# Scaling the inputs of two output projections by their RMS-norm factor ahead of the matmul, and adding the products to x from PSUM

## The chip, the cores and the metric

The kernel runs on one core of one Trainium2 chip. The metric is the device time of one execution in microseconds (us). The engines are PE (TensorE, matmul), DVE (VectorE), ACT (ScalarE), POOL (GpSimd) and SP (SyncE, which issues most DMAs).

## What is computed

The reference is one inference step of a decoder trunk with two layers, for a prompt of 512 tokens and 8 samples of 4 tokens (544 columns in all), with a model width of 1024. What matters here is the mixing part of a layer:

```python
a = window_attention(q, k_ext, v_ext, sinks, pos0)          # 512 wide
c = causal_depthwise(u_ext, w_dw, b_dw)                     # 512 wide
c = jax.nn.silu(layernorm(c, ln_g, ln_b)) @ w_pw2
mix = jnp.concatenate([rmsnorm(a, g_attn_out), rmsnorm(c, g_conv_out)], axis=-1) @ w_o
x = x + mix
x = x + jnp.square(jax.nn.relu(rmsnorm(x, g_ffn) @ w_up)) @ w_down
x = x + (p @ w_ple) * jax.nn.sigmoid(rmsnorm(x, g_ple) @ w_ple_gate)
```

An RMS norm multiplies every token by one factor, the reciprocal root of its mean square, and every feature by a gain. The factor of a token can be applied ahead of the matmul that follows or behind it, since the matmul sums over features only.

## The kernel before

Everything is held with features on the 128 partitions and the 544 tokens along the free dimension: x is eight tiles of 128x544, the attention output `aT` and the output `cn` of the pointwise product are four tiles each. The matmuls work in fp32r, and to keep fp32 accuracy each operand is split in a high and a low part; `split` (L584) makes a tile `pr` of both: ACT writes the high part (scaled by the gain, when one is given), DVE writes the rest. `group` (L567) multiplies one block of 128 output features by all input tiles: for each input tile three matmuls (high x high, high x low, low x high) for each of two halves of 288 and 256 columns, which accumulate in two PSUM banks. With four input tiles that is 24 matmuls. Weights are loaded 512 KB at a time by SP; ACT makes their high part and the negative of it, and a DMA issued by POOL adds the raw weights, or DVE subtracts (L493).

`rstd` (L613) makes the norm factor: the squares (ACT) are summed over tiles by DVE or POOL (`sqsum`, L594), PE sums over partitions with a matmul against ones, DVE scales (TENSOR_SCALAR t<-bank), POOL takes the power -0.5 (t<-t,mhalf), PE broadcasts the result over partitions (bank<-ident,t), and ACT copies it to a tile of 128x544 in two pieces (448 and 96 columns).

The stages of a layer that the change touches are, in the code: `an` (L954: splits of the four attention tiles with the gain, and the factor Ra), `oa` (L957: the projection of the attention half, eight groups), `ln` and `pw` (L966, L983: layer norm, SiLU, pointwise product, whose four groups give `cn`), `cn` (L991: splits of `cn` and the factor Rc), `oc` (L994: the projection of the convolution half, eight groups), and then `ffn` (L1003). In `oa` and `oc` each group's two banks are multiplied by the factor into a half tile (`mulR`, L683), and a further DVE addition of 128x544 adds the half tile to x. `addx` (L695) adds two banks to x directly; in this kernel nothing calls it yet.

The order of the instructions on each engine isn't the order of the code. `Program` (L155) records operations with their dependences and a duration, and `schedule` (L207) is a list planner: at each point in its own time it starts on every free engine the ready operation with the smallest key, if its buffers are free. The key is the place of the operation's section in `ORDERS` (L36, one list for each layer) and then the order of recording; evacuations of PSUM recorded while `first` is set go ahead of all others. An operation counts as ready 0.13 us after the last one that it depends on (L358). The chip then takes the planned order of each engine as it is. In layer 0 the list has pw and cn ahead of an, ln, ple and oa, with oc and ffn behind; in layer 1 it has ln and pw ahead of an, then cn, ple, oa, oc, ffn. Section ple is a product of a small embedding input with its own weights, independent of the rest of the layer.

Since every instruction is issued by one helper, all rows carry the line L1143, and groups are told apart by tile names: `pr` split inputs, `hfs` half tiles, `bank` PSUM, `raw`, `wh`, `wl` weights, `par` the gains, `fa`, `fb`, `fc`, `C`, `tq` and `hg` the forms of ffn, `t` small tiles.

Of the kernel before, what the change touches and what calls it, by code (L numbers as in the profile page):

```python
# [12 lines left out]
ALU = mybir.AluOpType  # L13
# [42 lines left out]
SQ = {"hr": "dd", "sp": [2, 4], "an": "pd", "ln": "dp", "cn": "pp"}  # L56
BC = {"hr": [0, 0], "an": [0, 0], "cn": [0, 0], "ffn": [0, 0], "gate": [0, 0]}
W0B = 1
ENG = {"d": "dve", "p": "pool", "m": "dma"}
KINDS = set(SLOTS) | {"hf"}  # L60

# [93 lines left out]
class Program:  # L155
# [51 lines left out]
    def schedule(self):  # L207
# [84 lines left out]
        t = 0.0  # L292
        left_ops = len(self.ops)
        while left_ops:
            while events and events[0][0] <= t:
                _, _, o = heapq.heappop(events)
# [5 lines left out]
            for e in engs:  # L302
                w, h = wait[e], heap[e]
                while w and w[0][0] <= t:
                    _, p, i, o = heapq.heappop(w)
# [15 lines left out]
                o = pick  # L321
# [33 lines left out]
                heapq.heappush(events, (o.end, id(o), o))  # L355
                for s in o.succ:
                    s.n -= 1
                    s.ready = max(s.ready, o.end + (0.0 if s.eng == e == "pe" else 0.13))  # L358
                    if s.n == 0:
                        heapq.heappush(wait[s.eng], (s.ready, s.key, id(s), s))  # L360
                progress = True
# [13 lines left out]
            t = min(nxt)  # L375
# [4 lines left out]
class Kernel:  # L380
# [131 lines left out]
    def quad(self, l, idx, F, how, taps):  # L512
# [10 lines left out]
        whole = slice(0, 1024)  # L523
        conv(p, whole, {4: a, 1: b}, ENG[how[0]])
        self.tt(p[:, a], p[:, a], q[:, a], ALU.add)
        self.tt(q[:, a], q[:, a], p[:, b], ALU.add)
        self.tt(p[:, b], p[:, b], p[:, a], ALU.add)
        conv(p, whole, {5: a, 6: b}, ENG[how[1]])
        conv(q, b, {2: b}, ENG[how[2]])
        self.tt(q[:, b], q[:, b], p[:, b], ALU.add)  # L530
        conv(q, whole, {7: a, 3: b}, ENG[how[3]])
        bank = {}
# [61 lines left out]
    def sqsum(self, tiles, cols=slice(0, T), parts=1, eng="d", split=0):  # L594
        def chain(ts, e):
            s = None
            for a in ts:
# [4 lines left out]
                else:  # L602
                    self.tt(s[:, cols], s[:, cols], q[:, cols], ALU.add, ENG[e])
            return s
# [75 lines left out]
    def record(self):  # L680
        i, o, pg = self.i, self.o, self.pg

        def mulR(out, pv, r):  # L683
            pg.first = EVAC
            for h in range(2):
                self.tt(out[:, HS[h]], pv[h], r[:, HS[h]], ALU.mult)
            pg.first = False
# [7 lines left out]
        def addx(xm, pv):  # L695
            pg.first = EVAC
            for h in range(2):
                self.tt(xm[:, HS[h]], pv[h], xm[:, HS[h]], ALU.add)
            pg.first = False

        def const(name, shape):
            t = self.fixed(shape, name)
            self.dma(t, i[name])
            return t
# [9 lines left out]
        x = [self.fixed([128, T], "x") for _ in range(KD)]  # L714
        self.dma(par[0][:, 0:8], i["par"][0][:, 0:8])
        first = [self.sb("raw", [128, 1024], F32, "raw") for _ in range(2)]
        after = {0: (0, 0), W0B: (0, 1), KD - 1: (1, 0)}
        for k in range(KD):
            self.dma(x[k], i["xT"][:, k, :])
            if k in after:  # L720
                n, c = after[k]
# [11 lines left out]
        for l in range(L):  # L733
            t = self.fixed([128, NH], "sinkp")
# [4 lines left out]
            t = self.fixed([128, 2], "sinks")  # L739
# [8 lines left out]
        for l in range(L):  # L748
            def sec(name):
                pg.sec(name, l)  # L750
# [3 lines left out]
            g_a, g_c, b_dw, ln_g, ln_b = (P[:, 24 + 4 * n:28 + 4 * n] for n in range(5))  # L754
# [19 lines left out]
            for c in range(4):  # L774
# [8 lines left out]
                t = self.hf()  # L783
# [68 lines left out]
            aT = []  # L852
            for t in range(4):
                sec(f"q{t}")
                q32 = rope(10 + t, 0.125)
                for g in range(2):
                    r = slice(64 * g, 64 * g + 64)
# [9 lines left out]
                for n in range(4):  # L867
# [4 lines left out]
                    for g in range(2):  # L872
                        if n % 2 == 0:
                            S[g] = self.ps1()
                        r = slice(64 * g, 64 * g + 64)
# [5 lines left out]
                for g in range(2):  # L881
# [3 lines left out]
                    for bp in range(2):  # L885
# [3 lines left out]
                        for d in range(nn):  # L889
                            blk, n = bp * 2 + d // 2, bp * 2 + d // 2 + d % 2  # L890
                            src = 0 if n == 0 else 2 * n - 1 + (blk - n + 1)
# [41 lines left out]
            for g in range(2):  # L933
                r = slice(64 * g, 64 * g + 64)
# [10 lines left out]
            for q in range(2):  # L945
                for w in self.weights(l, LD_PLE + q, 4, 2):
                    pv = self.group(w, pa)
                    t = self.hf()
# [3 lines left out]
                    pp.append(d)  # L952

            sec("an")  # L954
            aa = [self.split(aT[t], g_a[:, t:t + 1]) for t in range(4)]
            Ra = self.rstd(self.sqsum(aT, eng=SQ["an"][l]), 512, dma=BC["an"][l])
            sec("oa")  # L957
            for q in range(4):
                for m, w in enumerate(self.weights(l, LD_OA + q, 2, 4)):
                    pv = self.group(w, aa)  # L960
                    t = self.hf()
                    mulR(t, pv, Ra)
                    xm = x[2 * q + m]
                    self.tt(xm, t, xm, ALU.add)

            sec("ln")  # L966
            mu = self.ps2()
# [7 lines left out]
            for c in range(4):  # L975
                t = self.hf()
# [7 lines left out]
            cn = []  # L984
            for q in range(2):
                for w in self.weights(l, LD_PW + q, 2, 4):
                    pv = self.group(w, sa)
                    t = self.hf()
                    copy(t, pv)
                    cn.append(t)  # L990
            sec("cn")  # L991
            ca = [self.split(cn[c], g_c[:, c:c + 1]) for c in range(4)]
            Rc = self.rstd(self.sqsum(cn, eng=SQ["cn"][l]), DC, dma=BC["cn"][l])
            sec("oc")  # L994
            for q in range(4):
                for m, w in enumerate(self.weights(l, LD_OC + q, 2, 4)):
                    pv = self.group(w, ca)
                    t = self.hf()
                    mulR(t, pv, Rc)
                    xm = x[2 * q + m]  # L1000
                    self.tt(xm, t, xm, ALU.add)

            sec("ffn")  # L1003
            F, odd = {}, [None]
# [6 lines left out]
            for c in range(CHUNKS):  # L1011
                G = {}
                for k in range(4):
                    s, C = (self.sb("pair", [128, 4, TH], F32, n) for n in ("s", "C"))
# [52 lines left out]
            for hs in ((0,), (1,)) if last else ((0, 1),):  # L1067
                for m in range(8):
                    pv = self.group(ws[m] if last else self.weights(l, LD_GATE + m, 1, KD)[0], h, hs)
                    t = self.hf()  # L1070
# [205 lines left out]
```

## Time and profile before

| | us |
|---|---|
| median of 3 runs | 1254.72 |
| lowest and highest | 1251.88, 1254.75 |
| the profiled execution | 1254.24 |
| its span | 1252.5 |
| PE busy | 1205.1 |
| DVE busy | 1057.9 |
| ACT busy | 884.3 |
| POOL busy | 286.9 |

The mean granted clock of the profiled execution is 0.987. The span runs from the first to the last instruction; times in all rows below count from its start. A row of the groups gives engine, operation, output<-inputs, shapes and count, then busy time and the mean duration of one in ns, then the idle time of the engine ahead of it and what ended that. A row of the windows gives a stretch and its length, then busy time (and number of instructions) of PE, PEld, DVE, ACT and POOL (an engine without any is left out when the view is restricted to one tile), the granted clock, the share of the DMA engines and GB/s. A row of the time line gives start, duration, instruction and, in brackets, the idle time just before it and what ended it. Matmuls overlap in the pipeline: their mean duration is about 290 ns, but in a full stretch about 200 of them start in 25 us.

### The profile page before, as it was taken

The page shows a single profiled execution, that of the slowest core. Times are in us where ns is not written, and L with a number is a line of the kernel's source. Part 1 is how long each engine was busy: PE and PEld are TensorE (multiplying, and loading weights), DVE is VectorE, ACT ScalarE, POOL GpSimd, SP SyncE. Part 2 cuts the span into 40 slices and gives each one's busy share as a digit, 9 for nine tenths or more (in the row PEclk, how much of TensorE's full clock was granted, in tenths as well). Part 3 has the DMA queues.
Part 4 walks back from the last instruction along what each step waited for, and adds up shares of the span by engine and source line. Part 5 has one row for each costly group of instructions (what it writes and reads, how often), then busy time and mean ns, then how long its engine had stood idle before and what let it go on. Part 6 is the DMA issues. An engine that isn't in the chain of part 4 may idle for free.

```text
span 1252.5 us, 24414 instructions
## 1 busy us (share of the span) xinstructions
PE 1205.1 (96%) x9424; PEld 1177.4 (94%) x9424; DVE 1057.9 (84%) x2024; ACT 884.3 (71%) x1464; POOL 286.9 (23%) x296
## 2 busy tenths in 40 slices
PE   6998999999999999999999999999999999999997
PEld 6997899999999999999999979999999999999996
DVE  4999976999798897986559997798979979979855
ACT  7777886785775865857757688787758568577752
POOL 1747233110101101102147802201111011010111
PEclk8999999999999999999999999998999999999998
DMA  9895456285866858869979825535687587697862
GB/s 279 209 266 137 113 122 142 49 203 142 208 156 159 212 137 195 185 214 248 231 200 205 190 75 142 123 85 120 162 200 176 143 201 172 153 205 192 201 153 72
DMA packets 69701, 212.23 MB, mean 169 GB/s; under 512 B 11736, under 2 KB 16088, under 8 KB 69584
## 3 DMA queue, kind: packets, MB, share of 16 engines
q0 software_dynamic: 23328, 84.95, 36.6%
q1 hardware_dynamic: 46256, 125.72, 31.3%
q8 instruction: 74, 1.21, 0.4%
q14 instruction: 43, 0.35, 0.1%
HBM read 115.42 MB, written 10.28 MB: 100 GB/s over the span
## 4 chain that ended last, share of the span: by engine, by line
PE 48%; DVE 28%; issue 8%; DMA 8%; ACT 6%; POOL 1%; SPq 0%; DVEq 0%; POOLq 0%; ACTq 0%
PE bank L1143 48%; DVE bank L1143 6%; DMA wl<-raw 5%; DVE hfs L1143 5%; DMA raw<-wall 3%; DVE fb L1143 3%; DVE C L1143 3%; DVE raw L1143 2%; DVE tq L1143 2%; DVE wl L1143 2%; ACT wh L1143 2%; DVE x L1143 1%; ACT wl L1143 1%; DVE P L1143 1%; ACT hfs L1143 1%
## 5 line engine op out<-in xcount | busy, mean ns | idle before, releaser
L1143 PE MATMUL bank<-fb,wh 128*128 128x272 f32 x3072 | 585.6, 289 | 2.8 <-DVE fb L1143 1.7
L1143 PEld LDWEIGHTS bank<-fb,wh 128*128 128x128 f32 x3072 | 482.9, 189 | 5.8 <-DVE fb L1143 2.8
L1143 PE MATMUL bank<-fb,wl 128*128 128x272 f32 x1536 | 443.4, 289 | 8.4 <-DMA wl<-raw 5.7
L1143 ACT ACTIVATE wh<-raw 128x1024 fp32r<-128x1024 f32 (+1 forms) x326 | 312.7, 966 | 174.8 <-PE bank L1143 98.6
L1143 PE MATMUL bank<-pr,wh 128*128 128x256 f32 (+1 forms) x2176 | 425.1, 294 | 6.4 <-ACT wh L1143 6.0
L1143 PEld LDWEIGHTS bank<-pr,wh 128*128 128x128 f32 x2176 | 346.2, 191 | 11.7 <-ACT wh L1143 6.0
L1143 POOL DMA_DIRECT2D wl<-raw x162 | 141.1, 873 | 826.9 <-ACT wl L1143 610.4
L1143 PE MATMUL bank<-pr,wl 128*128 128x288 f32 (+1 forms) x1088 | 315.0, 290 | 1.3 <-DMA wl<-raw 1.3
L1143 PEld LDWEIGHTS bank<-fb,wl 128*128 128x128 f32 x1536 | 290.1, 189 | 10.1 <-DMA wl<-raw 6.8
L1143 PEld LDWEIGHTS bank<-pr,wl 128*128 128x128 f32 x1088 | 206.9, 190 | 1.9 <-DMA wl<-raw 1.7
L1143 DVE TENSOR_TENSOR wl<-raw,wh 128x1024 fp32r<-128x1024 f32 (+1 forms) x164 | 163.4, 998 | 23.5 <-PE bank L1143 15.0
L1143 ACT ACTIVATE wl<-raw 128x1024 fp32r<-128x1024 f32 x162 | 170.0, 1049 | 4.1 <-DVE raw L1143 4.0
L1143 DVE TENSOR_TENSOR raw<-raw,raw 128x512 f32<-128x512 f32 x192 | 130.8, 683 | 1.1
L1143 DVE SCALAR_TENSOR_TENSOR bank<-U,par,bank 128x512 f32<-128x512 f32 x176 | 126.9, 746 | 2.1 <-ACT bank L1143 0.8
L1143 DVE TENSOR_TENSOR x<-x,bank 128x272 f32<-128x272 f32 (+1 forms) x224 | 102.7, 470 | 29.5 <-PE bank L1143 29.0
L1143 POOL TENSOR_TENSOR hfs<-hfs,hfs 128x512 f32<-128x512 f32 (+3 forms) x74 | 101.0, 1367 | 48.7 <-ACT hfs L1143 23.0
L1143 PE MATMUL bank<-fa,wh 128*128 128x272 f32 x512 | 102.6, 292 | 1.7 <-DVE fa L1143 1.7
L1143 DVE TENSOR_TENSOR hfs<-bank,hfs 128x256 f32<-128x256 f32 (+2 forms) x160 | 65.9, 445 | 41.4 <-PE bank L1143 23.5
L1143 PEld LDWEIGHTS bank<-fa,wh 128*128 128x128 f32 x512 | 81.7, 190 | 3.3 <-DVE fa L1143 3.0
L1143 DVE TENSOR_TENSOR hfs<-hfs,hfs 128x544 f32<-128x544 f32 (+2 forms) x98 | 66.7, 685 | 17.1 <-ACT hfs L1143 16.2
L1143 ACT ACTIVATE hfs<-bank 128x288 f32<-128x288 f32 (+6 forms) x126 | 42.7, 379 | 45.9 <-PE bank L1143 45.0
L1143 PE MATMUL bank<-fa,wl 128*128 128x272 f32 x256 | 74.2, 290 | 0.0
(98 smaller groups left out, 1263.5 us busy)
## 6 DMA issues: line engine op xcount, KB each, us to landing
raw<-wall SPq DMA_DIRECT2D x194, 512.0 KB, 4.6
wl<-raw POOLq DMA_DIRECT2D x162, 512.0 KB, 5.7
pp<-hfs SPq DMA_DIRECT2D x16, 272.0 KB, 2.0
hfs<-pp SPq DMA_DIRECT2D x16, 272.0 KB, 8.4
x<-xT SPq DMA_DIRECT2D x8, 272.0 KB, 5.4
out_y<-hfs SPq DMA_DIRECT2D x8, 144.0 KB, 1.8
U<-stT SPq DMA_DIRECT2D x8, 136.0 KB, 4.5
out_conv_s<-U SPq DMA_DIRECT2D x8, 136.0 KB, 5.1
```

The source lines that it names most:

```text
L1143: getattr(getattr(nc, eng), method)(**{k: real(a) for k, a in {**outs, **ins}.items()})
```

## The change

The inputs of both projections are multiplied by gain and factor ahead of their splits, so that the splits need the factor; the banks are added to x directly. The planner gets a table of waiting times by engine, with 0.13 for each.

```diff
+SLACK = {"pe": 0.13, "act": 0.13, "dve": 0.13, "pool": 0.13, "sp": 0.13}
...
-                    s.ready = max(s.ready, o.end + (0.0 if s.eng == e == "pe" else 0.13))
+                    s.ready = max(s.ready, o.end + (0.0 if s.eng == e == "pe" else 0.13 if s.eng == e else SLACK[s.eng]))
...
+        def normed(src, g, r):
+            t = self.hf()
+            self.stt(t, src, g, r, ALU.mult, ALU.mult)
+            return self.split(t)
...
             sec("an")
-            aa = [self.split(aT[t], g_a[:, t:t + 1]) for t in range(4)]
             Ra = self.rstd(self.sqsum(aT, eng=SQ["an"][l]), 512, dma=BC["an"][l])
+            aa = [normed(aT[t], g_a[:, t:t + 1], Ra) for t in range(4)]
             sec("oa")
             for q in range(4):
                 for m, w in enumerate(self.weights(l, LD_OA + q, 2, 4)):
                     pv = self.group(w, aa)
-                    t = self.hf()
-                    mulR(t, pv, Ra)
-                    xm = x[2 * q + m]
-                    self.tt(xm, t, xm, ALU.add)
+                    addx(x[2 * q + m], pv)
...
             sec("cn")
-            ca = [self.split(cn[c], g_c[:, c:c + 1]) for c in range(4)]
             Rc = self.rstd(self.sqsum(cn, eng=SQ["cn"][l]), DC, dma=BC["cn"][l])
+            ca = [normed(cn[c], g_c[:, c:c + 1], Rc) for c in range(4)]
             sec("oc")
             for q in range(4):
                 for m, w in enumerate(self.weights(l, LD_OC + q, 2, 4)):
                     pv = self.group(w, ca)
-                    t = self.hf()
-                    mulR(t, pv, Rc)
-                    xm = x[2 * q + m]
-                    self.tt(xm, t, xm, ALU.add)
+                    addx(x[2 * q + m], pv)
```

## The prediction

> **What bounds the kernel now.** I read the page first: busy time by engine, then the chain that ended last.
>
> ```profile
> span 1252.5 us, 24414 instructions
> PE 1205.1 (96%) x9424; PEld 1177.4 (94%) x9424; DVE 1057.9 (84%) x2024; ACT 884.3 (71%) x1464; POOL 286.9 (23%) x296
> PE 48%; DVE 28%; issue 8%; DMA 8%; ACT 6%; POOL 1%; SPq 0%; DVEq 0%; POOLq 0%; ACTq 0%
> ```
>
> PE is busy 96% of the span and holds 48% of the chain. The second view is the table by windows of 25 us, for the stretches where each layer runs its two output projections (157 to 232 us, and 758 to 837 us).
>
> ```profile
> 150.00:175.00 25.00, 25.00 (x201) 23.67 (x200) 18.64 (x38) 22.85 (x53) 10.55 (x9) 1.00 0.40 99
> 175.00:200.00 25.00, 25.00 (x201) 24.75 (x200) 17.26 (x30) 21.69 (x36) 8.06 (x7) 1.00 0.68 154
> 200.00:225.00 25.00, 23.86 (x192) 23.62 (x192) 20.15 (x42) 15.13 (x26) 4.59 (x3) 1.00 0.45 108
> 775.00:800.00 25.00, 24.74 (x198) 24.17 (x197) 20.91 (x42) 16.07 (x24) 7.85 (x7) 1.00 0.68 169
> 800.00:825.00 25.00, 25.00 (x201) 24.72 (x201) 17.86 (x31) 18.13 (x34) 8.40 (x7) 1.00 0.48 106
> ```
>
> The columns after the length are PE, PEld, DVE, ACT and POOL busy time, then granted clock and DMA. In these stretches PE has about 200 matmuls per 25 us (0.124 us each) and no hole, while DVE has 4 to 8 us free in every 25. So PE bounds exactly the stages that the change touches. What PE eats there matters, and DVE time saved there is worth nothing directly.
>
> **What fills PE while the norm factor is being made.** Before the change the splits of the attention output need no factor, so the first projection's matmuls (their moving tile is pr) run while Ra is still being computed. The first two rows below are the windows view restricted to tile pr, the other two the same windows for everything.
>
> ```profile
> 160.00:176.00 16.00, 10.85 (x79) 9.94 (x78) 0.79 (x1) 0.78 (x1) 1.00 0.52 117
> 765.00:776.50 11.50, 8.01 (x58) 7.48 (x59) 0.78 (x1) 0.79 (x1) 1.00 0.72 155
> 160.00:176.00 16.00, 16.00 (x135) 15.39 (x134) 9.74 (x21) 13.95 (x24) 8.24 (x7) 1.00 0.52 117
> 765.00:776.50 11.50, 11.11 (x88) 10.43 (x85) 6.35 (x14) 9.91 (x15) 4.65 (x5) 1.00 0.72 155
> ```
>
> Of 16.00 us PE spends 10.85 on pr; of 11.50 us it spends 8.01. The rest (5.15 and 3.1 us) is the end of the last attention head, the sums over partitions and the broadcast of the factor. The pr matmuls of these windows cannot exist in the changed kernel before the factor does. When that is follows from the chain of Ra in layer 1 (time line of ACT, DVE, POOL):
>
> ```profile
> 766.42 0.64 ACT L1143 ACTIVATE hfs<-bank 128x512 f32<-128x512 f32 x1
> 767.85 0.79 ACT L1143 ACTIVATE pr<-hfs,par 128x544 fp32r<-128x544 f32 x1
> 768.49 0.70 ACT L1143 ACTIVATE hfs<-hfs 128x544 f32<-128x544 f32 x1
> 771.40 0.17 DVE L1143 TENSOR_SCALAR t<-bank 112x5 f32<-112x5 f32 x1 [1.31 <-PE bank L1143]
> 771.72 1.20 POOL L1143 TENSOR_TENSOR t<-t,mhalf 112x5 f32<-112x5 f32 x1 [0.43 <-DVE t L1143]
> 775.28 0.25 ACT L1143 ACTIVATE hfs<-bank 128x96 f32<-128x96 f32 x1 [0.34 <-PE bank L1143]
> ```
>
> The last attention tile is complete at 767.06, its square is 768.49 to 769.19, the power is on POOL to 772.92, and the last copy of Ra ends at 775.53. In layer 0 the last copy is this one:
>
> ```profile
> 175.42 0.23 ACT L1143 ACTIVATE hfs<-bank 128x96 f32<-128x96 f32 x1
> ```
>
> **The change part by part.** The prices come from the groups kept apart by shape.
>
> ```profile
> L1143 DVE TENSOR_TENSOR x<-hfs,x 128x544 f32<-128x544 f32 x32 | 25.1, 793 | 0.1
> L1143 DVE TENSOR_TENSOR hfs<-bank,hfs 128x288 f32<-128x288 f32 x76 | 33.6, 451 | 25.5 <-PE bank L1143 16.9 <-ACT hfs L1143 8.4
> L1143 DVE TENSOR_TENSOR x<-x,bank 128x272 f32<-128x272 f32 x192 | 80.6, 429 | 27.1 <-PE bank L1143 26.7
> L1143 DVE SCALAR_TENSOR_TENSOR C<-C,hfs 128x544 f32<-128x544 f32 x64 | 45.8, 718 | 3.2 <-ACT hfs L1143 2.6
> L1143 DVE SCALAR_TENSOR_TENSOR pr<-hfs,par,pr 128x544 fp32r<-128x544 f32 x16 | 13.0, 818 | 12.0 <-ACT pr L1143 12.0
> L1143 ACT ACTIVATE pr<-hfs 128x544 fp32r<-128x544 f32 x12 | 7.5, 647 | 0.0
> ```
>
> Evacuation: per group two products into a half tile (451 ns for 288 columns) become two additions into x from the bank (nearest row 429 ns for 272 columns). Equal, nothing on the path. The 32 separate additions to x go: 25.1 us of DVE.
>
> Inputs: 16 new products with gain and factor, priced by the nearest three-operand row at 0.72 us, so 11.5 us; the split behind them becomes a plain copy (0.65 us) and a subtraction (by the same 0.72 us, instead of 0.82). DVE ends 25.1 - 11.5 + 1.6 = 15 us lighter over both layers; none of that counts where DVE has holes.
>
> The planner's new table holds 0.13 in all five entries, the number that stood there: no effect.
>
> The wait in front of the first projection. Taking the split's ACT step out of the chain lets the last square run 0.64 us earlier, and then the product (0.72) and the copy (0.65) must pass before the first matmul: the first pr matmul comes about 0.7 us after the old end of Ra, so at 776.3 in layer 1 and, as ACT need not put its table load ahead of the last copy, at about 176 in layer 0. Those are the ends of my two windows. PE has nothing else that is ready there: ffn needs x, pw needs the layer norm. Matmuls that are not done there are done later, on an engine without holes, so each displaced microsecond counts. They are 10.85 us in layer 0. In layer 1 it is 8.01 us, and a second thing sets the end, below. Behind the waiting matmuls on PE's queue stand the matmuls of pw, and these wait for the layer norm's output themselves.
>
> The wait in front of the second projection. Its splits now also wait for their factor, Rc. Rows of layer 1: the last pw copies, the last square's sum on POOL, the copies of Rc, and the window of the second projection for tile pr; then, of layer 0, the last copy of pw, the copies of Rc, and the same window.
>
> ```profile
> 807.69 0.69 ACT L1143 ACTIVATE hfs<-bank 128x288 f32<-128x288 f32 x2
> 810.67 1.35 POOL L1143 TENSOR_TENSOR hfs<-hfs,hfs 128x544 f32<-128x544 f32 x1
> 817.41 0.66 ACT L1143 ACTIVATE hfs<-bank 128x448 f32<-128x448 f32 x2
> 808.20:835.00 26.80, 24.76 (x194) 24.20 (x192) 0.79 (x1) 0.78 (x1) 1.00 0.33 79
> 194.70 0.38 ACT L1143 ACTIVATE hfs<-bank 128x256 f32<-128x256 f32 x1
> 205.76 0.69 ACT L1143 ACTIVATE hfs<-bank 128x448 f32<-128x448 f32 x2 [7.60 <-PE bank L1143]
> 206.00:230.40 24.40, 24.36 (x195) 24.15 (x193) 0.00 (x0) 0.00 (x0) 1.00 0.38 87
> ```
>
> Rc exists at 818.07, ten microseconds after pw's last matmul. With the same 0.64 off and 0.72 + 0.65 on, the second projection can start at about 818.9 instead of 808.2, and needs its 24.76 us: end near 843.7 instead of 835.0, so +8.7. The 8.01 us of displaced first-projection work run inside that wait, so layer 1 costs the larger of the two, 8.7. In layer 0 the displaced 10.85 us cover it: the planner puts pw ahead, so its last copy still ends at 195.1 and those of Rc at 206.45, and the splits follow by about 207.2, while the first projection, which now ends at 206.0, keeps PE busy to 206.0 + 10.85 = 216.9. The cover has 9.7 us to spare; were pw later by more than that, the excess would be added.
>
> What comes back. After the second projection PE enters the head of ffn, where DVE is the late one:
>
> ```profile
> 230.40:290.00 59.60, 56.63 (x438) 54.79 (x437) 58.83 (x108) 45.40 (x75) 7.63 (x8) 1.00 0.56 133
> 835.00:898.00 63.00, 58.92 (x429) 56.85 (x427) 59.31 (x108) 45.95 (x75) 8.47 (x9) 0.95 0.60 138
> 853.50:860.20 6.70, 6.70 (x33) 6.70 (x33) 4.68 (x8) 2.40 (x3) 3.23 (x3) 0.50 0.81 147
> L1143 DVE TENSOR_TENSOR x<-hfs,x 128x544 f32<-128x544 f32 x8 | 5.7, 715 | 0.0
> ```
>
> DVE is full there (58.83 of 59.60), PE loses 3.0 and 4.1 us, and in layer 1 another 3.35 us because 6.70 us ran at clock 0.50. The last row counts 209 to 232.5 us: the eight additions that go are 5.7 us of DVE just ahead of that head, so DVE enters it lighter. At most the whole 10.4 us comes back, at least nothing; I take half, 5.2.
>
> **The clock.** A hole in PE can cost more than its length:
>
> ```profile
> 98.99 2.01 PE L1143 MATMUL bank<-hfs,swap 128*128 128x288 f32 x4 [4.86 <-ACT hfs L1143]
> 545.89 0.40 PE L1143 MATMUL bank<-fb,wl 128*128 128x272 f32 x1 [2.16 <-DMA wl<-raw]
> 540.00:553.00 13.00, 10.84 (x74) 10.62 (x74) 9.87 (x18) 6.64 (x9) 0.28 (x1) 0.87 0.92 288
> ```
>
> After 2.16 us of idling the clock's mean over 13 us is 0.87, so 0.13 x 13 / 0.5 = 3.4 us at half speed, 1.7 us lost. The new holes are longer (16 us with 5 us of small work). I take one such loss per layer, 3.4 us together; ends 0 and two per layer, 6.8.
>
> The Trainium skill ("TensorE: Matmul & The Clock Gate", Part 1 on the HAM clock gate) says that the clock halves only after at least one idle window of about 3.4 us and returns after one busy one. By that the small matmuls inside the holes might keep it up, and the sum would be 3.4 us lower, an estimate. The trace does not agree with the length: 2.16 us idle were enough.
>
> **The sum.** The profiled execution took 1254.24 us, of which 1252.5 is the span; the median of the three runs is 1254.72, so no correction between them is needed. 1254.2 + 10.9 + 8.7 + 3.4 - 5.2 = 1272.0 us. Its own range takes the ends: 1254.2 + 19.6 - 10.4 = 1263.4 and 1254.2 + 19.6 + 6.8 = 1280.6. About 0.3% (3.8 us) is what a measurement of this kernel can tell from no change.
>
> **The rivals.** Faster: the list planner finds other matmuls for both holes (it would have to hold back the groups of the embedding product that now end just ahead of the holes, whose inputs are ready early), and only the DVE relief remains: 1254.2 - 10.4 = 1243.8. It decides from the point where about 20 us of other pr matmuls lie inside the two waits. For it speaks that DVE is full in the heads; against it, that the planner runs whatever is ready at once, and that PE, full from 150 us on in the first of the windows above, leaves no such work over. Chance 0.12.
>
> Half hidden: 9.8 us of the holes are covered and all 10.4 come back: 1253.6, no change. Chance 0.10.
>
> Worse: the four products and four subtractions per projection, 4 x 1.44 = 5.8 us of DVE, land in front of layer-norm work, and in layer 1 pw and Rc come that much later, with two clock losses per layer: 1254.2 + 19.6 + 5.8 + 6.8 = 1286.4. For it: in layer 1 the products come due just as the layer norm's work starts on DVE. Against: the products that evacuated early banks in the same place are gone. Chance 0.16.
>
> **How the numbers follow.** The forecast has 0.62. Slower is 0.62 + 0.16 = 0.78, same 0.10, faster 0.12. The range runs from 1255, where half of the no-change case still counts, to 1287, which takes in the worse case: 0.62 + 0.16 + 0.05 = 0.83.
>
> **What would show it.** Right: no pr matmul between about 161 and 176, nor 765 and 776; the first projection's additions into x straight from the bank; second projection of layer 1 starting near 819; ffn starting about 11 and then, in all, 19 us later; half-clock windows right behind the holes; a shorter tail of DVE waits in the heads. Wrong: pr matmuls of another stage inside the waits, or heads of ffn that start at the old distance.

## The result and the profile after

The changed kernel takes 1273.73 us, the median of five runs (1272.1 to 1276.22), beside 1254.72 us for the kernel before in five runs (1251.88 to 1256.88). The ratio is 1.0155, with a 95% interval of 1.0136 to 1.0174: 19.0 us slower. The profiled execution took 1276.22 us, the longest of the five.

The page of the changed kernel, its span, its busy times and its chain by engine:

```profile
span 1274.5 us, 24383 instructions
PE 1214.8 (95%) x9424; PEld 1185.5 (93%) x9424; DVE 1048.7 (82%) x2008; ACT 882.8 (69%) x1464; POOL 285.0 (22%) x296
PE 38%; DVE 28%; DMA 11%; issue 11%; ACT 9%; POOL 1%; SPq 0%; DVEq 0%; POOLq 0%; ACTq 0%
```

DVE's busy time fell by 9.2 us and PE's count of instructions is the same, yet the span grew by 22.0 us, and PE's share of the chain that ended last went from 48% to 38%: waiting has come into a chain that PE's work held. Where it stands is seen in the windows of 25 us, the same columns as before:

```profile
150.00:175.00 25.00, 21.50 (x132) 19.79 (x131) 16.94 (x34) 18.19 (x47) 9.24 (x8) 0.77 0.49 129
175.00:200.00 25.00, 25.00 (x194) 25.00 (x194) 11.37 (x21) 19.99 (x32) 4.61 (x5) 0.96 0.34 68
775.00:800.00 25.00, 16.98 (x106) 15.48 (x104) 15.40 (x28) 14.61 (x27) 9.78 (x8) 0.73 0.64 160
800.00:825.00 25.00, 24.92 (x199) 24.70 (x198) 11.04 (x20) 21.39 (x35) 6.01 (x6) 1.00 0.30 65
```

In the first of them 132 matmuls ran instead of 201, in the third 106 instead of 198, and the mean clock there is 0.77 and 0.73 instead of 1.00. The windows behind are full again: what was missed is done later, not skipped.

To see what is lost and what is given back, I cut the span at PE's first and last matmul of a stage (from PE's time line in each kernel). The changed kernel was profiled a second time (label after_again), to tell the change from chance.

| stretch, us | before | after | after, again |
|---|---|---|---|
| start to ffn of layer 0 | 230.2 | 236.7 (+6.5) | 238.7 (+8.5) |
| ffn of layer 0 | 349.9 | 351.1 (+1.2) | 349.3 (-0.6) |
| to the end of layer 1's attention | 185.3 | 192.2 (+6.9) | 185.5 (+0.2) |
| from there to ffn of layer 1 | 69.4 | 80.4 (+11.0) | 81.5 (+12.1) |
| ffn of layer 1 | 355.9 | 352.7 (-3.2) | 356.0 (+0.1) |
| rest | 61.8 | 61.4 (-0.4) | 61.4 (-0.4) |
| span | 1252.5 | 1274.5 (+22.0) | 1272.4 (+19.9) |

The two stages with the projections cost 17.5 and 20.6 us in the two profiles. The 6.9 us between the layers in the first of them are not there in the second, so they are not the change's.

The hole of each layer in PE's time line of the changed kernel:

```profile
163.34 3.89 PE L1143 MATMUL bank<-ones,hfs 128*112 128x1 f32 x20 [2.76 <-POOL hfs L1143]
167.09 4.56 PE L1143 MATMUL bank<-ident,t 112*128 112x112 f32 x20
171.40 0.61 PE L1143 MATMUL bank<-pr,wh 128*128 128x288 f32 x1
783.78 1.32 PE L1143 MATMUL bank<-ones,hfs 128*112 128x1 f32 x10 [3.76 <-DVE hfs L1143]
784.99 2.18 PE L1143 MATMUL bank<-hfs,ones 128*128 128x288 f32 x4
786.96 2.29 PE L1143 MATMUL bank<-ident,t 112*128 112x112 f32 x10
793.51 2.03 PE L1143 MATMUL bank<-ones,hfs 128*112 128x1 f32 x10 [4.26 <-POOL hfs L1143]
795.40 0.83 PE L1143 MATMUL bank<-pr,wh 128*128 128x288 f32 x2
```

The attention's last matmul ends at 159.6 in layer 0 and at 780.0 in layer 1; the first of the projection (moving tile pr) starts 11.8 and 15.4 us later. Between them stand the last six matmuls of the embedding product in layer 0 (to 160.6), and otherwise only small chains: the sums over partitions, the layer norm's mean (bank<-hfs,ones) and the broadcasts of the factors. Layer 1's wait is the longer, and its last matmuls ahead of pr are ten sums (bank<-ones,hfs at 793.51) that waited 4.26 us for POOL. The same stretch on ACT, POOL and DVE says what they are:

```profile
790.29 0.24 ACT L1143 ACTIVATE hfs<-bank 128x96 f32<-128x96 f32 x1
788.95 4.51 POOL L1143 TENSOR_TENSOR hfs<-hfs,hfs 128x544 f32<-128x544 f32 x3 [2.29 <-ACT hfs L1143]
790.64 1.63 DVE L1143 SCALAR_TENSOR_TENSOR hfs<-hfs,par 128x544 f32<-128x544 f32 x1 [1.29 <-ACT hfs L1143]
792.30 0.66 ACT L1143 ACTIVATE pr<-hfs 128x544 fp32r<-128x544 f32 x1 [1.77 <-DVE hfs L1143]
792.99 1.05 DVE L1143 TENSOR_TENSOR pr<-hfs,pr 128x544 fp32r<-128x544 f32 x1 [0.72 <-ACT pr L1143]
```

The last copy of Ra ends at 790.53, the new product at 792.27, the new plain copy at 792.96. The first split input is there, and the projection could start; but the planner put the layer norm's sums over partitions ahead of it on PE, and these need POOL's additions, which end at 793.46. They run at half clock (2.03 us; 1.05 before), and pr starts behind them at 795.40.

The new work has these prices (groups by shape, changed kernel):

```profile
L1143 DVE TENSOR_TENSOR x<-bank,x 128x288 f32<-128x288 f32 x32 | 14.5, 453 | 29.3 <-PE bank L1143 29.1
L1143 DVE TENSOR_TENSOR x<-bank,x 128x256 f32<-128x256 f32 x32 | 13.3, 414 | 2.0 <-PE bank L1143 2.0
L1143 DVE SCALAR_TENSOR_TENSOR hfs<-hfs,par,hfs 128x544 f32<-128x544 f32 x13 | 9.9, 779 | 2.5 <-ACT hfs L1143 2.4
L1143 DVE SCALAR_TENSOR_TENSOR hfs<-hfs,par 128x544 f32<-128x544 f32 x3 | 3.2, 1065 | 1.3 <-ACT hfs L1143 1.3
```

An addition straight from the bank takes 453 ns where the product into the half tile took 451: nothing. The 16 products take 13.1 us instead of the 11.5 in the prediction.

Then the clock, and the heads of both ffn stages (windows, changed kernel):

```profile
163.50:177.10 13.60, 12.87 (x60) 12.55 (x61) 8.61 (x15) 6.86 (x13) 3.31 (x3) 0.50 0.54 138
784.60:798.10 13.50, 9.24 (x40) 8.45 (x40) 9.37 (x18) 5.49 (x10) 7.66 (x6) 0.50 0.68 169
236.70:296.30 59.60, 58.06 (x455) 56.72 (x454) 57.05 (x104) 44.96 (x76) 7.69 (x8) 1.00 0.59 141
860.40:923.40 63.00, 61.21 (x481) 59.87 (x480) 60.31 (x108) 47.06 (x77) 7.66 (x8) 1.00 0.57 134
```

In this profile PE runs at half clock for about 13.6 us in each layer, beginning just behind the first idle stretch. In the second profile it is 10.2 us in layer 0 (from 168.8) and twice 6.8 us in layer 1 (from 776.4 and 786.7). The heads get 455 and 481 matmuls done in the same length where before they got 438 and 429.

### The profile page after: what moved, and what is told of

Its sections match the earlier page's. It is cut to its first block, busy times and chain, and to the rows that moved or that the text cites. A ratio compares the mean times of both kernels' runs of the same rounds, so it can differ in the third digit from the quotient of the medians.

```text
span 1274.5 us, 24383 instructions
## 1 busy us (share of the span) xinstructions
PE 1214.8 (95%) x9424; PEld 1185.5 (93%) x9424; DVE 1048.7 (82%) x2008; ACT 882.8 (69%) x1464; POOL 285.0 (22%) x296
## 4 chain that ended last, share of the span: by engine, by line
PE 38%; DVE 28%; DMA 11%; issue 11%; ACT 9%; POOL 1%; SPq 0%; DVEq 0%; POOLq 0%; ACTq 0%
PE bank L1143 38%; DMA wl<-raw 7%; DVE bank L1143 5%; DMA raw<-wall 4%; DVE hfs L1143 4%; DVE raw L1143 3%; DVE C L1143 3%; DVE wl L1143 3%; DVE fb L1143 3%; ACT hfs L1143 3%; DVE x L1143 2%; DVE tq L1143 2%; ACT wh L1143 2%; DVE P L1143 1%; ACT wl L1143 1%
## 5 line engine op out<-in xcount | busy, mean ns | idle before, releaser
L1143 PE MATMUL bank<-pr,wh 128*128 128x256 f32 (+1 forms) x2176 | 429.5, 296 | 7.2 <-ACT wh L1143 6.0
L1143 PEld LDWEIGHTS bank<-pr,wh 128*128 128x128 f32 x2176 | 350.5, 193 | 12.9 <-ACT wh L1143 6.0
L1143 DVE TENSOR_TENSOR wl<-raw,wh 128x1024 fp32r<-128x1024 f32 (+1 forms) x164 | 162.8, 996 | 22.0 <-ACT wh L1143 9.9
L1143 POOL TENSOR_TENSOR hfs<-hfs,hfs 128x512 f32<-128x512 f32 (+3 forms) x72 | 98.4, 1369 | 36.3 <-DVE t L1143 16.1
L1143 ACT ACTIVATE hfs<-bank 128x288 f32<-128x288 f32 (+6 forms) x126 | 42.6, 379 | 55.2 <-PE bank L1143 53.5
L1143 DVE TENSOR_TENSOR hfs<-bank,hfs 128x288 f32<-128x288 f32 (+2 forms) x96 | 41.1, 454 | 34.4 <-PE bank L1143 19.0
```

What stands on the lines that cost most here:

```text
L1143: getattr(getattr(nc, eng), method)(**{k: real(a) for k, a in {**outs, **ins}.items()})
```

## The experiments

The theory: the wait for the factor costs all of the loss, because PE's work that used to fill it comes later on an engine without holes; the direct addition is worth little. The rivals: the new DVE work or the order in the heads costs it; or the two projections add; or the clock makes up much of it.

### Each projection alone

In the first kernel only the projection of the attention half is changed, in the second only that of the convolution half. The edit of the first, against the changed kernel; the second does the same to `aa` and Ra:

```diff
+            ca = [self.split(cn[c], g_c[:, c:c + 1]) for c in range(4)]
             Rc = self.rstd(self.sqsum(cn, eng=SQ["cn"][l]), DC, dma=BC["cn"][l])
-            ca = [normed(cn[c], g_c[:, c:c + 1], Rc) for c in range(4)]
...
-                    addx(x[2 * q + m], pv)
+                    t = self.hf()
+                    mulR(t, pv, Rc)
+                    xm = x[2 * q + m]
+                    self.tt(xm, t, xm, ALU.add)
```

> Only the first projection (oa) takes its factor ahead of the split and is added to x from PSUM; the second (oc) is as before. Waits in front of the matmuls as the cause: layer 0 keeps its whole delay (7.8 us in the changed kernel's trace), layer 1 loses the 8 us of displaced matmuls and about 1.4 us at half clock, so 1268 to 1274 us, nearly the whole change. Rival, that the cost is shared evenly by the two projections: about 1264 us.

> Only the second projection (oc) takes its factor ahead of the split; oa is as before. Waits as the cause: in layer 0 about 1 to 2 us (the splits come about 1.2 us after the first projection ends), in layer 1 about 10.7 us plus 1 to 2 us at half clock, so 1264 to 1270 us; and the costs of the two halves, taken alone, add up to more than the 19 us of the whole change, because in layer 1 one wait runs inside the other. Rival, that the costs add: the two halves sum to 19 us.

Measured: 1273.04 us (1270.21 to 1273.65), ratio 1.0149 [1.013, 1.0168], and 1273.15 us (1271.43 to 1273.68), ratio 1.0152 [1.0135, 1.0169], the kernel before at 1254.31 in the same batch. Each alone costs 18.7 and 18.8 us, both together 19.0: the totals do not add, and the second was dearer than I expected. By stage, the first takes +6.0 ahead of ffn in layer 0 and +13.0 in layer 1, as the whole change does. The second takes +2.4 and +12.6, and 10.2 us more inside layer 0's ffn, where PE waits 5.6 us for a single POOL operation (its row stands further down) and runs at half clock for 10.2 us; layer 1's ffn is 5.7 us shorter. So it is chance that both totals are near 19. By stage, layer 0 fits adding (6.0 and 2.4 beside 6.5 and 8.5 for both together), and it is layer 1 that doesn't add (13.0 and 12.6 beside 11.0 and 12.1). In layer 1 the second kernel shows a wait of its own (PE's time line of oc_only):

```profile
824.46 1.39 PE L1146 MATMUL bank<-ones,hfs 128*112 128x1 f32 x10 [3.48 <-POOL hfs L1146]
827.99 2.45 PE L1146 MATMUL bank<-ident,t 112*128 112x112 f32 x10 [2.15 <-POOL t L1146]
832.32 0.61 PE L1146 MATMUL bank<-pr,wh 128*128 128x288 f32 x1 [1.88 <-ACT pr L1146]
```

The first projection ends at 821.0 and the second starts at 832.3: the 11.3 us that Rc needs. In the whole change this hole is not there; the second projection follows the first at once (836.4). So in layer 1 only one of the two waits counts, and there it is that for Ra.

### The direct addition without the wait

The splits use the gain only, as before, and the banks are added to x directly. Both norm factors are still computed but applied nowhere, so the result lacks them.

```diff
+            aa = [self.split(aT[t], g_a[:, t:t + 1]) for t in range(4)]
             Ra = self.rstd(self.sqsum(aT, eng=SQ["an"][l]), 512, dma=BC["an"][l])
-            aa = [normed(aT[t], g_a[:, t:t + 1], Ra) for t in range(4)]
...
+            ca = [self.split(cn[c], g_c[:, c:c + 1]) for c in range(4)]
             Rc = self.rstd(self.sqsum(cn, eng=SQ["cn"][l]), DC, dma=BC["cn"][l])
-            ca = [normed(cn[c], g_c[:, c:c + 1], Rc) for c in range(4)]
```

> Splits as before with the gain alone, banks added to x directly; Ra and Rc are computed and applied nowhere, so both norm factors are left out of the result. Without waits only the lighter DVE is left: 1250 to 1254 us if the relief is worth up to 5 us. Rival, that adding from PSUM is itself a cost (banks now wait for x): above 1256 us.

Measured: 1253.76 us (1251.91 to 1262.13), ratio 1.0008 [0.9988, 1.0027]: no difference. Its windows:

```profile
150.00:175.00 25.00, 25.00 (x202) 23.61 (x201) 19.38 (x40) 22.88 (x54) 11.41 (x10) 1.00 0.40 100
775.00:800.00 25.00, 24.85 (x201) 24.63 (x200) 13.23 (x27) 15.88 (x25) 7.10 (x6) 1.00 0.63 158
```

PE is full and at full clock, as before. DVE has 13.23 us of work in the second window where it had 20.91, and nobody is faster for it. Without the waits, the direct addition brings nothing that can be measured.

### The wait without the direct addition

The kernel before, with one edit: no matmul of a projection may be planned ahead of the last copy of its factor. `split`, products and additions are the old ones.

```diff
+        self.hold = []
...
-        deps = {id(a): a for a in after}
+        deps = {id(a): a for a in list(after) + (self.hold if eng == "pe" else [])}
...
             Ra = self.rstd(self.sqsum(aT, eng=SQ["an"][l]), 512, dma=BC["an"][l])
+            Rop = pg.ops[-1]
...
+                    pg.hold = [Rop]
                     pv = self.group(w, aa)
+                    pg.hold = []
```

The same three lines stand around the second projection with Rc. A further kernel (label held_direct) holds the matmuls in the same way in the kernel of the section above, so it has the wait and the direct addition, but no work between factor and matmul; again both factors are left out of the result.

> The kernel before, with splits, factors, evacuation and additions as they were; only the planner may not place the matmuls of the two projections before the last copy of Ra (Rc). That leaves PE with the same wait and DVE with its early splits. If the wait on PE is the cost: 1272 to 1279 us, as the changed kernel. Rival, that the splits which come late on DVE are the larger part of it (as the 1296.8 us of the variant with the old evacuation may mean): below 1264 us.

> Splits with the gain alone, banks added to x directly, both factors left out of the result, and the planner may not place the projections' matmuls before the last copy of Ra (Rc). Early splits, the wait, the direct addition. If the direct addition is worth something wherever PE has waited: 1255 to 1262 us. If it only pays for the DVE work that late splits push against the second projection: near the held kernel with the old evacuation, 1270 to 1276 us.

Measured: the held kernel 1275.1 us (1272.84 to 1276.79), ratio 1.0147 [1.0122, 1.0172], 18.7 us over its batch's 1256.38. The wait alone has the size of the whole change. With the direct addition it is 1268.66 us (1266.42 to 1272.39), ratio 1.0111 [1.0081, 1.0142], in neither of the two expected ranges: about 6 us come back by the medians, though the intervals of the two ratios overlap. The waits and the heads of the held kernel (windows):

```profile
165.00:175.10 10.10, 7.19 (x41) 7.10 (x41) 4.39 (x9) 6.67 (x11) 5.56 (x5) 0.71 0.37 70
773.90:785.60 11.70, 6.00 (x25) 5.46 (x25) 6.69 (x15) 7.84 (x12) 3.78 (x4) 0.62 0.77 169
238.60:298.20 59.60, 56.60 (x438) 54.80 (x437) 58.83 (x108) 45.48 (x75) 7.64 (x8) 1.00 0.56 133
857.20:920.20 63.00, 60.12 (x465) 58.14 (x465) 62.23 (x114) 47.84 (x78) 7.61 (x8) 1.00 0.53 126
298.20:358.20 60.00, 60.00 (x481) 60.00 (x480) 51.49 (x89) 40.52 (x57) 8.62 (x10) 1.00 0.73 180
```

The holes (10.1 and 11.7 us) and the low clock over them (0.71 and 0.62) are of the same kind as in the changed kernel (11.8 and 15.4 us, 0.66 and 0.65). The heads separate what DVE's relief does: layer 0 has 438 matmuls as before, against 455 in the changed kernel; layer 1 has 465, against 481. So the relief is worth 17 and 16 matmuls, 2.1 and 2.0 us at 0.124 us each. The held kernel with direct additions, whose planned waits are the same, has 456 and 480. The other 36 of layer 1 (429 to 465) came without any relief: before's head held 6.70 us of half clock, this one holds none (27 of the 36, by an estimate from 3.35 us at 0.124). The 6 us of the direct addition stand elsewhere: in the two profiles, layer 1's stretch ahead of ffn is 78.4 us instead of 83.1, where the held kernel has a second gap between pr matmuls (788.0 to 791.7) and the other has none.

### The late inputs without the direct addition

The inputs are scaled ahead of the splits as in the change, but each bank goes into the half tile, multiplied by ones, and is added to x from there:

```diff
+        def mul1(out, pv):
+            pg.first = EVAC
+            for h in range(2):
+                self.tt(out[:, HS[h]], pv[h], ones[:, 0:1].bc(128, HW[h]), ALU.mult)
+            pg.first = False
...
-                    addx(x[2 * q + m], pv)
+                    t = self.hf()
+                    mul1(t, pv)
+                    xm = x[2 * q + m]
+                    self.tt(xm, t, xm, ALU.add)
```

The same lines stand in the second projection.

> Factor ahead of the splits in both projections, but each bank is still taken in two steps on DVE, times a tile of ones into a half tile and then added to x. Waits as the cause, with little relief: 1274 to 1279 us. Rival, that the direct addition gives back 10 us or more of a larger cost: above 1283 us.

Measured: 1296.76 us (1294.55 to 1298.74), ratio 1.0344 [1.0319, 1.0368]. I missed this one; the rival had it. Its stages ahead of ffn are 1.7 and 1.4 us longer than in the changed kernel, its two ffn stages 11.1 and 11.8 (362.2 and 364.5 us). The windows of the second projection and of the head, layer 0, then PE's time line:

```profile
214.00:238.50 24.50, 24.48 (x195) 24.26 (x194) 24.50 (x49) 17.46 (x29) 0.92 (x1) 1.00 0.12 22
238.40:298.00 59.60, 51.87 (x372) 50.57 (x371) 51.93 (x92) 42.60 (x69) 7.63 (x8) 0.91 0.55 129
```

```profile
253.80 0.59 PE L1155 MATMUL bank<-fb,wl 128*128 128x272 f32 x1 [4.22 <-DVE wl L1155]
```

The same stretch of the kernel before, in the same view:

```profile
206.20:230.40 24.20, 24.20 (x195) 24.20 (x195) 21.04 (x43) 19.67 (x33) 1.78 (x2) 1.00 0.38 88
```

DVE is full through the whole second projection (24.50 of 24.50; 21.04 of 24.20 before), and the low parts of ffn's weights, which DVE also makes, are late: 372 matmuls in the head instead of 455. With late splits the direct addition is therefore worth 23 us; without them it is worth nothing (no wait) or about 6 us that the intervals don't separate (held kernels). It is not the wait that fills DVE: the held kernel has the wait and the old additions, and its head does as many matmuls as before, 438. It is the late splits together with the old additions.

### Which wait sets the end

Two kernels: six copies of a factor onto itself by ACT stand behind its `rstd`, of Ra in the first, of Rc in the second; each takes 0.69 us, six 4.1 us. The computation is the same.

```diff
             Ra = self.rstd(self.sqsum(aT, eng=SQ["an"][l]), 512, dma=BC["an"][l])
+            for _ in range(6):
+                self.act(Ra, Ra, AF.Copy)
```

> The changed kernel with six copies of Ra onto itself (ACT, about 4 us) between the factor and the products that need it. If the wait for Ra sets the end in both layers: about 4 us in each, 1280 to 1284 us. If, as predicted, the wait for Rc sets it in layer 1: 4 us in layer 0 alone, 1276 to 1279 us.

> The same six copies, on Rc. If the first projection's displaced matmuls cover the wait for Rc in both layers (by the changed kernel's trace they last about 4 us longer than it): 1274 to 1277 us. If the wait for Rc sets the end in layer 1: 4 us more, 1278 us or above.

Measured: Ra later 1278.86 us (1277.75 to 1279.46), ratio 1.0189 [1.0163, 1.0214]. In the trace both layers move: ffn starts at 243.5 instead of 236.7 and 238.7 in layer 0, and the stretch of layer 1 is 84.6 us instead of 80.4 and 81.5. The total lies in the rival's range, because layer 1's ffn took 348.3 us, 4.4 less than the change's. The trace speaks for the theory, the total does not settle it.

Rc later: 1292.44 us (1288.09 to 1295.39), ratio 1.0295 [1.0255, 1.0335], 18.7 us more than the change. The theory's range failed; the rival's lower bound holds, but the rival had nothing of this size. The second projection ran out of cover: the first copied input of it was there at 832.4 in the changed kernel and PE began at 836.4, so 4.0 us were to spare (2.4 us for its low part, there at 834.0), and 4.1 us of copies used them up: PE now idles ahead of the second projection, and the stages of the two layers are 2.4 and 4.9 us longer than in the change's first profile. Most of the loss is behind them, in ffn: 6.1 and 9.5 us. PE's, POOL's and DVE's time line there, in layer 0 of this kernel:

```profile
254.97 2.25 PE L1145 MATMUL bank<-ident,t 112*128 112x112 f32 x10 [4.77 <-POOL t L1145]
248.34 6.57 POOL L1145 TENSOR_TENSOR t<-t,mhalf 112x5 f32<-112x5 f32 x1
248.11 0.43 DVE L1145 TENSOR_TENSOR C<-bank,s 128x272 f32<-128x272 f32 x1
248.46 0.68 DVE L1145 TENSOR_TENSOR raw<-raw,raw 128x512 f32<-128x512 f32 x1
253.21 0.68 DVE L1145 TENSOR_TENSOR raw<-raw 128x512 f32<-128x512 f32 x1
```

and the same power on POOL in the changed kernel:

```profile
245.90 1.57 POOL L1143 TENSOR_TENSOR t<-t,mhalf 112x5 f32<-112x5 f32 x1 [14.69 <-DVE t L1143]
```

A power of 112x5 elements takes 6.57 us instead of 1.57. From 248.46 to 253.89 DVE runs additions and subtractions on SBUF tiles (raw, wl) without a gap, and POOL is done 1.02 us after the last of them. In layer 1 of this kernel it is 6.58 us, in the kernel with Rc's wait alone (layer 0, the 10.2 us above) 6.91; everywhere else this operation takes 0.7 to 3.6 us. ffn's norm factor waits for it, and PE for the factor, 4.8 us in each layer. What the rest of the loss in ffn is, these rows do not show.

### The wait filled, and other work put into it

Two attempts to fill the hole. In the first, 26 groups of three matmuls, whose result nobody reads, may run from the last attention tile on, to keep the clock up. In the second, the matmuls of the embedding product (section ple), which now end ahead of the hole, are held back until the last attention tile. Both use the `hold` of the held kernel.

```diff
+                atop = pg.ops[-1]
...
+            sec("gate")
+            dw, pg.hold = self.ps1(), [atop]
+            for _ in range(26):
+                self.mm([(dw[:, 0:256], pa[0][:, 0, 0:128], pa[0][:, 0, 0:256], True, True)] * 3)
+            pg.hold = []
```

```diff
+                atop = pg.ops[-1]
...
+                    pg.hold = [atop]
...
+                    pg.hold = []
```

> The changed kernel with 26 groups of three matmuls per layer that nobody reads, held until the last attention tile is complete and placed where PE has nothing else, so that its clock stays up during the first wait. If the half clock behind and inside the wait (13.7 us in each layer) is a part of the cost: 1266 to 1270 us. Rival, that the clock costs nothing beyond the wait or that the filler's own time eats it: 1273 us or more.

> The changed kernel with the matmuls of the embedding product held until the last attention tile is complete, so that they fall into the first wait. If PE's work is conserved, a hole opens among the attention matmuls instead: 1270 to 1276 us. Rival, that such cover was there to be had: 1262 us or less.

Measured: with fillers 1271.66 us (1270.35 to 1276.45), ratio 1.0128 [1.0098, 1.0158]; with the product held 1269.27 us (1266.38 to 1275.17), ratio 1.0094 [1.0066, 1.0123]. The windows of the two waits with fillers:

```profile
160.20:174.20 14.00, 14.00 (x108) 13.86 (x107) 6.76 (x13) 8.34 (x17) 5.36 (x5) 0.88 0.67 171
772.00:787.90 15.90, 14.77 (x110) 13.99 (x106) 8.30 (x15) 9.09 (x16) 7.36 (x6) 0.89 0.85 209
```

The clock is 0.88 and 0.89 over the waits, and layer 0's projections take 62.6 us from first to last matmul instead of 65.5. But the fillers stand in the way of the factor's own matmuls (the broadcasts start at 169.0 instead of 167.1, and the wait is 14.0 us instead of 11.8), and the total lies between the two expected ranges, its interval over both: the clock is worth 2.9 us in layer 0 behind the wait, and what it is worth in all stays open. Of the held product, the window that it left (held_ple):

```profile
125.00:150.00 25.00, 18.74 (x127) 14.00 (x125) 24.24 (x92) 18.98 (x62) 3.73 (x7) 0.86 0.37 85
```

PE is now idle for 6.26 us there; in the changed kernel it is 1.40 us (23.60 busy). The old wait is filled (PE is busy for all of 159.9 to 180.0), but the hole has moved ahead by some 30 us. The median is just below the range that I gave for that, and far from the rival's.

### A second profile, and the layer norm's sums moved

> The changed kernel once more, for a second profile. If the 6.9 us that its first profile lost between the end of the first ffn and the second layer's attention belong to the planned order, they are there again within 2 us; if they are chance (the clock's windows), they are mostly gone.

The table above has it: 1274.15 us, and the 6.9 us between the layers were gone (185.5 us against 192.2 and 185.3). The last kernel takes the sums that stood ahead of pr in layer 1 from POOL to DVE:

```diff
-SQ = {"hr": "dd", "sp": [2, 4], "an": "pd", "ln": "dp", "cn": "pp"}
+SQ = {"hr": "dd", "sp": [2, 4], "an": "pd", "ln": "dd", "cn": "pp"}
```

> The changed kernel with layer 1's sum of squares for the layer norm on DVE instead of POOL. In the trace of the changed kernel the first product with Ra took 1.63 us there instead of 0.78, with POOL additions running beside it. If that contention is a part of layer 1's wait: 1 to 3 us less, 1271 to 1273 us. Rival, nothing: 1274 us.

Measured: 1269.01 us (1264.8 to 1273.0), ratio 1.0111 [1.0074, 1.0147]. The wait of layer 1 is 14.7 us instead of 15.4 and 16.0, and the stage to ffn 81.2 us, as it was: what it was meant to shorten hardly moved. The product took 0.78 us instead of 1.63, so the contention is gone, but Ra's last copy ends 11.2 us after the attention instead of 10.5, and the sums, now behind DVE, still stand ahead of pr on PE (783.34 to 785.37; pr starts at 785.23). The lower total is not explained by it, and the intervals overlap, so I take nothing from it. No version that applies both factors beats the kernel before.

## Why the prediction was right, point by point

**PE bounds the stages and nothing covers the waits: right.** The wait without any other edit costs 18.7 us, the direct addition without the wait nothing that can be measured. The projection's matmuls are missing where I said so, though the edges differ: from 160.6 to 171.4 in layer 0 (said: 161 to 176), and in layer 1, which as a whole comes later, for the 15.4 us behind the attention (said: about 11). The embedding product, held back, only moved the hole.

**Displaced work of layer 0, 10.85 us, and 1.7 of clock: right in kind, too large.** The stage grew by 6.5 and 8.5 us, not 12.6. I let the first pr matmul start at 176, where Ra's old end was. It starts at 171.4 (173.3 in the second profile). The pr matmuls that went had also stood between the last ones of the attention and of the factor itself: the attention ends at 159.6 and 162.8 instead of 163.4, and the factor follows without them. The chain's end came sooner once the work that stood between its links was gone.

**Layer 1, the larger of 8.01 and 8.7, and 1.7 of clock: right in size, wrong in cause.** The stretch grew by 11.0 and 12.1 us where I had 10.4. But I named Rc's wait as the one that sets the end, and it was the first projection's. The step that failed is "the first pr matmul comes about 0.7 us after the old end of Ra", so 10.9 us after the attention's end; it came 15.4 us after it. The rows above split these 4.5 us (to 0.1): Ra's last copy ends 10.5 us after the attention where I had 9.5 (the small matmuls at half clock take back more than the 0.64 us that I had saved); product and copy with their gaps take 2.4 us instead of 1.4, as the product ran 1.63 us beside POOL's additions; and 2.4 us are the layer norm's sums ahead of pr on PE. This split is read from the rows; no run puts pr ahead of the sums with nothing else changed. I had asked what stands behind the waiting matmuls, and not what the planner would put ahead of them. And Rc was no fixed time: pw is planned by what is ready, so it moved with the attention's end, and Rc came in with 4.0 us to spare. The second projection starts 56.4 us after the attention's end, where my 818.9 would have been 53.5. Rc's own price was right: alone it makes a hole of 11.3 us where I had 10.7 (818.9 against 808.2).

**The cover of Rc in layer 0, "9.7 us to spare": right that it covers, wrong in size.** The second projection follows the first without a hole, but the first split input is ready at 208.8 and PE gets to it at 212.7: 3.9 us, because the first projection ended earlier than I had it. Rc 4.1 us later ate this up.

**The clock, 3.4 us: right in sign, small.** I had one loss per layer from 3.4 us at half speed; it was 13.6 us per layer in both layers of the first profile, and 10.2 and 13.6 in the second, of which much fell on waiting. What it slows is the small matmuls of the chain (2.03 us for ten sums, 1.05 before) and the first 5.7 us of the projection in layer 0. By the rule that I had quoted from the Trainium skill ("TensorE: Matmul & The Clock Gate", Part 1), that the clock halves only after at least one idle window of about 3.4 us, the small matmuls might have kept it up; they did not, and layer 0's idle stretch in front of them is 2.76 us.

**What comes back, 5.2 us: the step that failed most.** The heads did run faster, by 2.1 and 2.0 us from the relief (measured against the held kernel). But ffn as a whole kept none of it in layer 0 (+1.2 and -0.6), and in layer 1 -3.2 and +0.1, where the held kernel without relief has -3.6. Layer 1's two values are the clock: before had 6.7 us at half clock in that ffn (its row stands in the prediction), the second profile 6.8 us (the row below), the first none.

```profile
1172.40:1179.20 6.80, 5.89 (x26) 5.89 (x27) 2.67 (x4) 1.81 (x3) 0.00 (x0) 0.50 0.61 206
```

With half of each taken off, an estimate, the three are 352.6, 352.7 and 352.6 us: by that, nothing came back in layer 1. In layer 0, in the 60 us behind the head, PE's waits in the changed kernel (us in all, times, longest) show one that neither before nor the held kernel has:

```profile
PE bank L1143 <- DMA wl<-raw: 1.3, 1, 1.3
```

PE is through the head sooner and then waits for the transfer of weights; the second profile, and the two kernels with direct additions but no factor, have the same wait with 1.4, 1.2 and 1.3 us. Over the whole ffn, PE's waits for these transfers are 2.8 and 2.9 us in the two layers before, the same in the held kernel, 4.0 and 5.1 in the changed one, 4.2 and 6.3 in its second profile. So time that the head gains turns in part into waiting for weights. That this takes all of the gain back is not shown: the kernel with the layer norm's sums on DVE has direct additions too, and waits 2.6 and 3.8 us.

**The sum.** The parts that I had too large (layer 0 by 4 to 6 us) and the part that didn't come back (3 to 5 us) nearly cancel, and layer 1 was 0.6 to 1.7 us dearer than I had it. That the total came out 1.7 us from the forecast is luck. The total alone would have confirmed a wrong story of layer 1.

**The worse rival's place was real.** It had DVE's new work landing in front of other work. The change is free of that by little: with the old additions in place DVE is full and the two ffn stages lose 23 us, and with Rc 4.1 us later they lose most of 18.7.

## What to carry to other kernels

Scaling the input of a matmul instead of its output moves a reduction from behind the matmul to in front of it; on an engine that is full, the price is the work that used to run during that reduction and can't be done elsewhere, and here the time saved on an engine with holes did not pay for it. When two waits are put into one stage, work out when the second's input comes with the first wait in place, and look at what the planner puts ahead of the waiting instructions as well as behind them. Check a total that fits by stage, with a second profile of the same kernel.

## What the runs showed of the hardware

A POOL operation of 112x5 elements took 6.57, 6.58 and 6.91 us, where in ffn it otherwise takes 1.2 to 2.2, while DVE ran operations on SBUF tiles back to back, and it ended 1.0 to 1.1 us after DVE's run of them did. The Trainium skill ("SBUF — State Buffer", the section on SBUF's two separate sides) says that a DVE instruction with two inputs in SBUF and a GpSimd instruction that reads SBUF share a pair of ports, and that whichever starts first keeps it for the whole instruction while the other blocks. The trace agrees that POOL is held up, and it fits POOL getting no turn between DVE's instructions during 5.4 us; which of them came first it does not settle, since POOL's record starts 0.12 us ahead of the run in the row above. No run was made to alter this alone, so it is read from three rows. In the other direction a product on DVE took 1.63 us beside POOL's additions, and 0.78 where they had gone to DVE.

In the first profile of the changed kernel the clock fell to 0.50 after idle stretches of 2.76 and 3.76 us that were followed by small matmuls, and stayed there for 13.6 us, although PE shows 12.87 us busy of these in layer 0. In the second it stayed there for 10.2 us in layer 0 and for two times 6.8 us in layer 1.
